# First half's final rows between products, row factors in two steps, and the second half's output projection in one piece

## The chip, the cores and the metric

The kernel runs on one core of a Trainium2 chip. The metric is the device time of one execution in microseconds (us). In the texts PE is the matrix engine (TensorE), PEld its loading of stationary operands, DVE the vector engine, ACT the scalar engine, POOL GpSimd, and SP the engine whose queue issues nearly all DMAs. A name such as L1216 is a line of the kernel before.

## What is computed

One step of a decoder layer on 1024 prompt tokens and 64 sample tokens (8 sequences of 8), 1088 tokens in all, with 1024 features, in float32:

```
xn   = rmsnorm(x, g_mix);  proj = xn @ w_in
S, o_g = gla_chunked(...)              # 4 heads of gated linear attention, 512 columns
o_g  = rmsnorm(o_g, g_gla) * silu(r)
o_s  = dilated_prompt(...) / dilated_sample(...)   # 8 softmax heads, 512 columns
h    = x + concat([o_g, o_s]) @ w_out              # w_out is 1024 x 1024
hn   = rmsnorm(h, g_ffn)
y    = h + (silu(hn @ w_fg) * (hn @ w_fu)) @ w_fd  # hidden width 2816
out  = rmsnorm(y, g_final)
```

States and caches are returned too; the change doesn't touch them.

## The kernel before

Every float32 product is made of three products of operands that are split into a high part (ACT copies with rounding, L172) and a low part (DVE subtracts, L173): hi by hi, lo by hi and hi by lo. So each weight that arrives by DMA takes an ACT and a DVE instruction before PE can use it. Tokens lie in the columns of products. They are cut into halves of 544 and pieces of `NH` = 272.

The order of instructions on each engine is not the order in which they are written. A scheduler places them by its own estimate of when operands are there and by priorities: `tc.high_priority()` pulls work forward, `fill_now` and `fill_behind` push work back by `LOW`. Buffers belong to rings: `pool.tile(..., tag=..., bufs=n)` hands out n buffers in turn, and the next user of a buffer waits until the last reader of the one before is done. Within an engine, instructions run in order, so that one that waits holds all that stands behind it. The names at each stage:

- **The filler.** `stream()` is a generator that yields after every group of products. First come 264 steps of six products of the input projection; then the GLA half of the output projection (rows 0 to 511 of w_out, L477 loads two column blocks of 128 at a time), in 48 steps of six products: 8 feature blocks, three token pieces of 384, 384 and 320 (`CHUNKS`), two steps each. Their sum with x goes back to `x_dram` in DRAM (L518, L519), through a ring `xa` of four. `FILL_AT` says how many steps are to be done at the end of each of the four attention pairs, and `FILL_ALL` how many there are.
- **The attention pairs** (`attn_pair`, four of them, the last from about 595 us). PE's own work for a pair is a chain through ACT and DVE; the steps of the filler stand between. The filler's 48 output steps all run from 600 to 705 us.
- **`out_half(hf)`** adds rows 512 to 1023 of w_out for one half of the tokens. It reads the attention output from `o_dram` (`load_rows`, L1027), splits it, takes four loads of w_out, and for 8 feature blocks by two token pieces makes 12 products into a bank of PSUM, which DVE adds to `xa`, read back from `x_dram` (L1041, L1046). For half 0 the sum stays in SBUF as `h[0]`, for half 1 it goes back to `x_dram`.
- **`factors(hf, ...)`** makes the row factors of the RMS norm: five products with one column (L1065), a chain of small DVE operations (`rms`, `rsqrt`), a broadcast into `rows`, five transposes on PE (L1073) and two copies into `rstd_bc`. `norm_half(hf)` multiplies h by them and builds the sums and splits `xhi`, `xlo` (tiles `B` and `T`) that the gate products read.
- **The 22 rounds** (`calls`, 11 of each half): `gate_up` makes seven blocks M1 to M7 of 24 products each (L1216, into banks `ps_a`, `ps_b`, `ps_c`), for which `gate_up_weights` loads four raw weight tiles A11, A21, A22, A12 and has POOL make the sums S1 to S4 (L1104), all out of the ring `raw` of seven buffers of 4 KB for each partition; `down` makes 96 products (L201 to L203, `ps_d`) and DVE adds them to `h`. The weights of `down` (`wd_raw`) use the single buffer `wraw`.
- **`final_rows(hf, t0, m)`** writes the final norm of 128 tokens: eight transposes of h into `ps_y` (a bank of the two of `ps_b`, L1294), a copy to `y` by ACT (L1295), the sum of squares by ACT (L1297), twelve small DVE operations on `st`, a product by DVE (L1299) and the DMA (L1300). `y` is the single buffer `wraw`. The first half's five calls stand behind the whole twelfth round, as does the load of `h[1]` (L1344).

Of the kernel before, what the change touches and what calls it, by code (L numbers as in the profile page):

```python
# [11 lines left out]
F32 = mybir.dt.float32  # L12
F32R = mybir.dt.float32r
# [6 lines left out]
P = 128  # L20
D = 1024
KT = D // P
# [16 lines left out]
FILL_AT = (156, 199, 242, 273, 306)  # L39
# [4 lines left out]
FILL_ALL = 312  # L44
# [59 lines left out]
def hymba_layer(  # L104
# [32 lines left out]
    def bank(tag):  # L137
        return psum.tile([P, 512], F32, tag=tag, name=f"ps_{tag}", bufs=1 if tag in "AX" else 2)
# [319 lines left out]
    def load_o(pl, c, half):  # L458
        c0, n = CHUNKS[c]
        hi = pl.tile([P, 4, 384], F32R, tag="ohi", name="ohi", bufs=3)  # L460
        lo = pl.tile([P, 4, 384], F32R, tag="olo", name="olo", bufs=3)
        oraw = pl.tile([P, 4, 384], F32, tag="oraw", name="oraw", bufs=2)
        dma(out=oraw[:, :, :n], in_=o_dram[512 * half : 512 * half + 512, c0 : c0 + n].rearrange("(k p) t -> p k t", p=P))
        for k in range(4):
            split(hi[:, k, :n], lo[:, k, :n], oraw[:, k, :n])
        return [hi[:, k, :n] for k in range(4)], [lo[:, k, :n] for k in range(4)]
# [17 lines left out]
    def stream():  # L484
# [21 lines left out]
        os = [load_o(outg, c, 0) for c in range(3)]  # L506
        for f in range(KT):
            if f % 2 == 0:
                ws, after = after, load_w_out(f + 2, 0) if f + 2 < KT else None
            for c, (c0, n) in enumerate(CHUNKS):  # L510
                cs = slice(c0, c0 + n)
                xa = outg.tile([P, 384], F32, tag="xa", name="xa", bufs=4)[:, :n]
                dma(out=xa, in_=x_dram[:, f, cs])
                ps = bank("mm")[:, :n]
                for k in (0, 2):
                    mm3(ps, [part[k : k + 2] for part in ws[f % 2]], [o[k : k + 2] for o in os[c]], first=k == 0, last=k == 2)
# [505 lines left out]
    def load_rows(c0):  # L1022
        hi = outp.tile([P, 4, NH], F32R, tag="ohi", name="ohi", bufs=4)
        lo = outp.tile([P, 4, NH], F32R, tag="olo", name="olo", bufs=4)
        for k in range(0, 4, 2):
            oraw = outp.tile([P, 2, NH], F32, tag="oraw", name="oraw", bufs=3)
            dma(out=oraw, in_=o_dram[512 + k * P : 512 + (k + 2) * P, c0 : c0 + NH].rearrange("(k p) t -> p k t", p=P))  # L1027
            split(hi[:, k : k + 2], lo[:, k : k + 2], oraw)
        return [hi[:, k] for k in range(4)], [lo[:, k] for k in range(4)]

    def out_half(hf):
        os = [load_rows(2 * NH * hf + NH * n) for n in range(2)]
        sq_acc = outp.tile([P, 2 * NH], F32, name="acc") if hf == 0 else None
        for f in range(KT):
            if f % 2 == 0:
                ws = load_w_out(f, 1)
            for n in range(2):
                cs = slice(NH * n, NH * n + NH)
                xs = x_dram[:, f, 2 * NH * hf + NH * n : 2 * NH * hf + NH * n + NH]
                xa = outp.tile([P, NH], F32, tag="xa", name="xa", bufs=3)  # L1040
                dma(out=xa, in_=xs)  # L1041
                ps = bank(("mm", "S", "T")[(2 * f + n) % 3])[:, :NH]
                mm3(ps, ws[f % 2], os[n])
# [5 lines left out]
                if hf:  # L1049
                    pass  # L1050
                elif f == 0:
                    act(out=sq_acc[:, cs], in_=row, func=AF.Square)
                else:
                    sq = outp.tile([P, NH], F32, tag="sq", name="sq", bufs=2)
                    act(out=sq, in_=row, func=AF.Square)
                    pool.tensor_tensor(out=sq_acc[:, cs], in0=sq_acc[:, cs], in1=sq, op=ALU.add)
        return sq_acc

    def factors(hf, sq_acc, ps, rb):
# [11 lines left out]
        vec.tensor_copy(out=rows, in_=st[:, 1, :].unsqueeze(2).broadcast_to([P, len(tiles), P]))  # L1071
        for j, m in tiles:
            nc.tensor.transpose(out=rb[j // 4][:, j % 4 * P : j % 4 * P + m], in_=rows[:m, j, :], identity=ident[:m, :m])  # L1073
# [100 lines left out]
    def gate_up(xs, own, following, wd):  # L1174
# [33 lines left out]
        for j, (name, _, slot, bk, first) in enumerate(ORDER):  # L1208
# [63 lines left out]
    factors(0, sums, bank("A"), [bank("X"), bank("A")])  # L1272
# [11 lines left out]
    def final_rows(hf, t0, m):  # L1284
# [3 lines left out]
        y = wpool.tile([P, KT, P], F32, tag="wraw", name="y", bufs=1).rearrange("p (f k) c -> p f (k c)", f=2)  # L1288
# [12 lines left out]

    calls = [(hf, i) for hf in range(2) for i in range(NF // 2)]
# [8 lines left out]
    for call, (hf, i) in enumerate(calls):  # L1311
        following = gate_up_weights(calls[call + 1][1]) if call + 1 < len(calls) else None
        B = gate_up(xs, own, following, load)
# [26 lines left out]
        if (hf, i) == (1, 0):  # L1340
            for t0 in range(0, 2 * NH, P):
                final_rows(0, t0, min(P, 2 * NH - t0))
            h[1] = residual()
            dma(out=h[1], in_=x_dram[:, :, 2 * NH :])  # L1344
# [96 lines left out]
```

## Time and profile before

| | us |
|---|---|
| median of 3 runs (lowest, highest) | 1628.04 (1627.64, 1631.65) |
| the profiled execution | 1630.76 |
| its span | 1629.0 |
| PE busy in the span | 1490.5 |
| DVE, ACT, POOL busy | 987.9, 590.3, 584.1 |
| mean granted clock of PE | 0.958 |

A busy time of PE counts matmuls that overlap, and a matmul at the lower clock counts for longer, so that 92% of the span is not 92% of what PE can do. More is learned from stretches of the span: which engine is busy in each, what the granted clock was, and for what PE waited there. The profile's rounds of the steady part are 33.2 us long and PE never stops in them; the rest of the text is about the stretches where it does.

### The profile page before, as it was taken

The numbers are of one execution on the slowest core, as the hardware profiler recorded it, in microseconds if no ns is written. First come the engines' busy times: TensorE is split into PE (matmuls) and PEld (weight loads), VectorE is DVE, ScalarE is ACT, GpSimd is POOL, SyncE is SP. The second block draws the span as 40 slices with busy tenths as digits, with TensorE's granted clock in tenths as the row PEclk, the third lists the DMA queues.
The fourth block names the chain that finished last, engine by engine and source line by source line (L and its number), as shares of the span: only waits on it lengthen the run. The fifth ranks groups of instructions, "written<-read, shape, count | busy, mean of one in ns | idle before, by whom it ended". The sixth has DMA issues, their size and how long they took to land.

```text
span 1629.0 us, 32149 instructions
## 1 busy us (share of the span) xinstructions
PE 1490.5 (92%) x13363; PEld 1338.2 (82%) x13363; DVE 987.9 (61%) x1673; ACT 590.3 (36%) x1002; POOL 584.1 (36%) x413
## 2 busy tenths in 40 slices
PE   7979999999999998978699999999884799999995
PEld 6867877887676766778589999999884799999995
DVE  5495675633323243246586787776975577767755
ACT  3243332243433444223443433333343243333432
POOL 1493332131121000033684453544642155544521
PEclk9988999999999999989799999999997899999997
DMA  4320021263534466575342322332413323323301
GB/s 151 102 71 27 25 67 43 56 197 105 141 103 123 123 182 197 163 239 175 110 144 78 102 81 87 108 92 78 133 53 119 107 91 106 102 79 104 91 27 55
DMA packets 237746, 172.58 MB, mean 106 GB/s; under 512 B 17792, under 2 KB 224032, under 8 KB 237600
## 3 DMA queue, kind: packets, MB, share of 16 engines
q1 hardware_dynamic: 233392, 170.31, 34.9%
q8 instruction: 105, 1.72, 0.4%
q10 hardware_dynamic: 4208, 0.21, 0.2%
q14 instruction: 41, 0.34, 0.1%
HBM read 144.79 MB, written 25.69 MB: 105 GB/s over the span
## 4 chain that ended last, share of the span: by engine, by line
PE 71%; DVE 12%; DMA 9%; ACT 2%; POOL 2%; issue 2%; SPq 1%; ACTq 0%; DVEq 0%; POOLq 0%
PE ps_b L1216 11%; PE ps_a L1216 6%; PE ps_c L1216 6%; PE ps_mm L201 6%; PE ps_mm L203 6%; PE ps_mm L202 6%; PE ps_d L201 5%; PE ps_d L203 5%; PE ps_d L202 5%; PE ps_S L840 2%; DMA x_dram<-xa 2%; DVE wlo L173 2%; PE ps_X L982 1%; PE ps_T L938 1%; DMA out_dram<-y 1%
## 5 line engine op out<-in xcount | busy, mean ns | idle before, releaser
L1104 POOL TENSOR_TENSOR raw<-raw 128x1024 f32<-128x1024 f32 x88 | 260.1, 2964 | 433.7 <-DVE wlo L173 280.1
L172 ACT ACTIVATE whi<-raw 128x1024 fp32r<-128x1024 f32 x154 | 162.9, 1058 | 240.3 <-PE ps_a L1216 87.0
L173 DVE TENSOR_TENSOR wlo<-raw,whi 128x1024 fp32r<-128x1024 f32 x154 | 242.2, 1575 | 0.0
L201 PE MATMUL ps_d<-ghi,wdhi 128*128 128x272 f32 (+2 forms) x704 | 205.5, 294 | 16.3 <-ACT wdhi L172 9.4
L202 PE MATMUL ps_d<-glo,wdhi 128*128 128x272 f32 (+2 forms) x704 | 205.6, 293 | 1.1 <-DVE glo L173 1.1
L201 PE MATMUL ps_mm<-xhi,whi 128*128 128x384 f32 (+1 forms) x576 | 199.4, 347 | 2.0 <-ACT whi L172 1.6
L203 PE MATMUL ps_d<-ghi,wdlo 128*128 128x272 f32 (+2 forms) x704 | 201.2, 292 | 0.0
L203 PE MATMUL ps_mm<-xhi,wlo 128*128 128x384 f32 (+1 forms) x576 | 195.1, 340 | 1.0 <-DVE wlo L173 1.0
L202 PE MATMUL ps_mm<-xlo,whi 128*128 128x384 f32 (+1 forms) x576 | 195.1, 339 | 0.2 <-DVE xlo L278 0.2
L1216 PE MATMUL ps_b<-xhi,whi 128*128 128x272 f32 x528 | 156.7, 297 | 18.5 <-ACT y L1295 11.3
L1216 PE MATMUL ps_b<-xhi,wlo 128*128 128x272 f32 x528 | 158.1, 299 | 5.6 <-DVE wlo L173 5.6
L1216 PE MATMUL ps_b<-xlo,whi 128*128 128x272 f32 x528 | 156.2, 296 | 2.4 <-DVE xlo L173 2.4
L201 PEld LDWEIGHTS ps_d<-ghi,wdhi 128*128 128x128 f32 x704 | 135.1, 192 | 18.2 <-ACT wdhi L172 11.6
L202 PEld LDWEIGHTS ps_d<-glo,wdhi 128*128 128x128 f32 x704 | 135.8, 193 | 1.5 <-DVE glo L173 1.5
L203 PEld LDWEIGHTS ps_d<-ghi,wdlo 128*128 128x128 f32 x704 | 133.4, 192 | 0.0
L201 PEld LDWEIGHTS ps_mm<-xhi,whi 128*128 128x128 f32 x576 | 110.7, 192 | 12.2 <-issue 7.3
L1216 PEld LDWEIGHTS ps_b<-xhi,whi 128*128 128x128 f32 x528 | 103.4, 196 | 20.2 <-ACT y L1295 11.8
L1266 DVE TENSOR_TENSOR h<-h,ps_d 128x544 f32<-128x544 f32 x168 | 113.7, 711 | 9.8 <-PE ps_d L203 9.8
L1216 PE MATMUL ps_a<-xhi,whi 128*128 128x272 f32 x352 | 102.7, 292 | 16.2 <-DVE xa L1046 10.1
L203 PEld LDWEIGHTS ps_mm<-xhi,wlo 128*128 128x128 f32 x576 | 110.4, 192 | 7.3 <-issue 5.3
L202 PEld LDWEIGHTS ps_mm<-xlo,whi 128*128 128x128 f32 x576 | 110.9, 193 | 6.3 <-issue 5.3
L1216 PEld LDWEIGHTS ps_b<-xhi,wlo 128*128 128x128 f32 x528 | 103.3, 196 | 7.9 <-DVE wlo L173 6.9
(363 smaller groups left out, 3453.2 us busy)
## 6 DMA issues: line engine op xcount, KB each, us to landing
raw<-in_w_ffn_gate_dram SPq DMA_DIRECT2D x88, 256.0 KB, 3.1
raw<-in_w_ffn_up_dram SPq DMA_DIRECT2D x88, 256.0 KB, 3.4
wd_raw<-in_w_ffn_down_dram SPq DMA_DIRECT2D x44, 512.0 KB, 3.8
wraw<-in_w_in_dram SPq DMA_DIRECT2D x22, 512.0 KB, 3.8
raw<-in_cache_swa_k_dram SPq DMA_DIRECT2D x32, 256.0 KB, 4.8
raw<-in_cache_swa_v_dram SPq DMA_DIRECT2D x32, 256.0 KB, 3.6
wraw<-in_w_out_dram SPq DMA_DIRECT2D x12, 512.0 KB, 4.0
xa<-x_dram SPq DMA_DIRECT2D x32, 136.0 KB, 2.7
```

The source lines that it names most:

```text
L172: a = by.tensor_copy(out=hi, in_=raw) if by else act(out=hi, in_=raw, func=AF.Copy)
L173: return a, vec.tensor_tensor(out=lo, in0=raw, in1=hi.bitcast(F32), op=ALU.subtract)
L201: mm(out=ps, lhsT=whi[k], rhs=xhi[k], start=first and k == 0, stop=False)
L202: mm(out=ps, lhsT=whi[k], rhs=xlo[k], start=False, stop=False)
L203: mm(out=ps, lhsT=wlo[k], rhs=xhi[k], start=False, stop=last and k == n - 1)
L840: ins = mm(out=out, lhsT=qres[own, qi * P + 32 * r : qi * P + 32 * r + 32], rhs=rhs, start=True, stop=True)
L938: nc.tensor.transpose(out=ps[:, r * P : (r + 1) * P], in_=raw[:, r, :], identity=ident)
L982: mm(out=av[rs, b2 * P : (b2 + 1) * P], lhsT=pT[:, t, rs], rhs=vts[b2][:, r, :], start=False, stop=t == 5 and b2 == 1)
L1104: add = lambda out, a, b, op: pool.tensor_tensor(out=out, in0=raw[a], in1=raw[b], op=op)
L1216: mm(out=banks[bk][:, s], lhsT=l[:, k, s], rhs=r, start=first and k == 0 and a == 0, stop=k == n - 1 and a == 2, skip_group_check=not first)
L1266: ins = vec.tensor_tensor(out=hk, in0=hk, in1=ps, op=ALU.add)
```

## The change

1. The filler's output steps cover only the first half of the tokens: two pieces of 272 instead of three, so 32 steps instead of 48 (`FILL_ALL` 312 to 296, `FILL_AT` with it). Its ring `xa` grows from four to six.
2. `out_half(1)` contracts all 1024 rows of w_out in one go: 24 products into a bank instead of 12, w_out by eight loads of 128 columns (`load_w`) instead of four of half the rows and 256 columns. `out_half`'s `xa` ring grows from three to six, and the tiles of `load_rows` are pairs in rings of nine.
3. `factors` ends with the broadcast `rows`; the transposes and copies are a new function `spread`. For the second half `factors` is called behind round 5 (counted from 0) and `spread` behind round 6.
4. `y` of `final_rows` comes from the ring `raw` of seven. The first half's final rows are called between the blocks of the second half's first two rounds: behind blocks 1, 3 and 5 of round 11, and behind blocks 0 and 2 of round 12; `h[1]` is loaded behind block 3 of it.

The diff, cut to its core:

```diff
-FILL_AT = (156, 199, 242, 273, 306)
+FILL_AT = (156, 194, 230, 264, 288)
-FILL_ALL = 312
+FILL_ALL = 296
...
-        os = [load_o(outg, c, 0) for c in range(3)]
+        os = [load_o(outg, n, 0) for n in range(2)]
...
-            for c, (c0, n) in enumerate(CHUNKS):
-                cs = slice(c0, c0 + n)
-                xa = outg.tile([P, 384], F32, tag="xa", name="xa", bufs=4)[:, :n]
+            for n in range(2):
+                cs = slice(NH * n, NH * n + NH)
+                xa = outg.tile([P, NH], F32, tag="xa", name="xa", bufs=6)
...
+    def load_rows(c0, ks):
+        pairs = []
+        for k in ks:
+            hi = outp.tile([P, 2, NH], F32R, tag="ohi", name="ohi", bufs=9)
+            lo = outp.tile([P, 2, NH], F32R, tag="olo", name="olo", bufs=9)
+            oraw = outp.tile([P, 2, NH], F32, tag="oraw", name="oraw", bufs=2)
...
+        os = [load_rows(2 * NH * hf + NH * n, range(0 if hf else 4, KT, 2)) for n in range(2)]
...
-            if f % 2 == 0:
-                ws = load_w_out(f, 1)
+            if hf:
+                parts = load_w(w_out[:, f * P : (f + 1) * P])
+                w = [[part[:, k] for k in range(KT)] for part in parts]
+            else:
+                if f % 2 == 0:
+                    ws = load_w_out(f, 1)
+                w = ws[f % 2]
...
-                xa = outp.tile([P, NH], F32, tag="xa", name="xa", bufs=3)
+                xa = outp.tile([P, NH], F32, tag="xa", name="xa", bufs=6)
...
-    def factors(hf, sq_acc, ps, rb):
+    def factors(hf, sq_acc, ps):
...
+        return rows
+
+    def spread(hf, rows, rb):
...
+            if j in between:
+                between[j]()
...
-        y = wpool.tile([P, KT, P], F32, tag="wraw", name="y", bufs=1).rearrange("p (f k) c -> p f (k c)", f=2)
+        y = ffp.tile([P, KT * P], F32, tag="raw", name="y", bufs=7).rearrange("p (f c) -> p f c", f=2)
...
-        B = gate_up(xs, own, following, load)
+        B = gate_up(xs, own, following, load, {
+            NF // 2: {j: lambda t=t: final_rows(0, P * t, P) for t, j in enumerate((1, 3, 5))},
+            NF // 2 + 1: {0: lambda: final_rows(0, 3 * P, P), 2: lambda: final_rows(0, 4 * P, 2 * NH - 4 * P), 3: next_rows},
+        }.get(call, {}))
...
         if call == 5:
+            factor_rows = factors(1, sums, psum2.tile([P, 2, 512], F32, tag="b", name="ps_f", bufs=2)[:, 0])
+        if call == 6:
             ps = psum2.tile([P, 2, 512], F32, tag="b", name="ps_f", bufs=2)
-            factors(1, sums, psum2.tile([P, 2, 512], F32, tag="b", name="ps_f", bufs=2)[:, 0], [ps[:, 0], ps[:, 1]])
+            spread(1, factor_rows, [ps[:, 0], ps[:, 1]])
```

How the change moves instructions is seen at three places. The first is DVE at the end of `out_half(1)`, where `xa<-ps` are the additions of the output projection (L1046, now L1053), `xlo` the low parts of the operands of the gate products, and `wlo` those of weights (from `raw`, for the gate; from `wraw`, for the output projection). Before:

```order
L1046 TENSOR_TENSOR xa<-ps_T,xa 128x272
L1168 SCALAR_TENSOR_TENSOR B<-h,gf,rstd_bc 128x2x272
L1168 SCALAR_TENSOR_TENSOR B<-h,gf,rstd_bc 128x544
L1046 TENSOR_TENSOR xa<-ps_mm,xa 128x272
L173 TENSOR_TENSOR xlo<-T,xhi 128x1088
L173 TENSOR_TENSOR xlo<-B,xhi 128x816
L1287 MEMSET st 128x4 x2
L1354 MEMSET one 128x1
L1389 MEMSET st_last 128x12
L173 TENSOR_TENSOR wlo<-raw,whi 128x1024
L173 TENSOR_TENSOR wdlo<-wd_raw,wdhi 128x1024
L173 TENSOR_TENSOR xlo<-T,xhi 128x1088 x2
```

After:

```order
L173 TENSOR_TENSOR xlo<-T,xhi 128x1088
L1053 TENSOR_TENSOR xa<-ps_S,xa 128x272
L173 TENSOR_TENSOR wlo<-wraw,whi 128x1024
L1053 TENSOR_TENSOR xa<-ps_T,xa 128x272
L173 TENSOR_TENSOR xlo<-T,xhi 128x1088
L1053 TENSOR_TENSOR xa<-ps_mm,xa 128x272
L173 TENSOR_TENSOR wlo<-wraw,whi 128x1024
L1053 TENSOR_TENSOR xa<-ps_S,xa 128x272
L173 TENSOR_TENSOR wlo<-raw,whi 128x1024
L1053 TENSOR_TENSOR xa<-ps_T,xa 128x272
L1053 TENSOR_TENSOR xa<-ps_mm,xa 128x272
L173 TENSOR_TENSOR wlo<-raw,whi 128x1024
```

Before, four low parts `xlo` stand behind the last addition of the output projection; after, four additions stand behind the last `xlo`.

The second is ACT in the second half's first rounds, where `y<-ps_y` and `T,st<-y` are the copy and the squares of final rows, `s<-ps_a` belongs to block M1, `B<-` to the blocks behind it, and `whi` to weights. Before:

```order
L1186 ACTIVATE s_13414<-ps_a 128x544
L172 ACTIVATE ghi<-B 128x544
L172 ACTIVATE whi<-raw 128x1024
L1295 ACTIVATE y<-ps_y 128x1024
L1297 ACTIVATE T,st<-y 128x1024
L1295 ACTIVATE y<-ps_y 128x1024
L1297 ACTIVATE T,st<-y 128x1024
L172 ACTIVATE whi<-raw 128x1024
L1295 ACTIVATE y<-ps_y 32x1024
L1297 ACTIVATE T,st<-y 32x1024
```

After:

```order
L1306 ACTIVATE y<-ps_y 128x1024
L1189 ACTIVATE B<-u_13127 128x272
L1308 ACTIVATE T,st<-y 128x1024
L172 ACTIVATE whi<-raw 128x1024 x2
L1189 ACTIVATE B<-s_13126 128x272
L1306 ACTIVATE y<-ps_y 128x1024
L172 ACTIVATE ghi<-B 128x544 x2
L1308 ACTIVATE T,st<-y 128x1024
L1306 ACTIVATE y<-ps_y 128x1024
L172 ACTIVATE whi<-raw 128x1024
L1195 ACTIVATE s_13454<-ps_a 128x544
L1308 ACTIVATE T,st<-y 128x1024
```

Before, three of the final rows' copies come in one run, with their squares and a single weight split between them; after, splits and blocks' copies stand between one copy and the next, and squares no longer follow their copy at once.

The third is the DMA queue (SP) at the same place: `out_dram<-y` are the final rows, `h<-x_dram` the load of the second half, `raw` and `wd_raw` weights. Before:

```order
L1102 DMA raw<-in_w_ffn_gate_dram 128x4x128
L1102 DMA raw<-in_w_ffn_up_dram 128x4x128
L1300 DMA out_dram<-y 128x1024
L1344 DMA h<-x_dram 128x8x544
L1300 DMA out_dram<-y 128x1024 x2
L1102 DMA raw<-in_w_ffn_gate_dram 128x4x128
L1102 DMA raw<-in_w_ffn_up_dram 128x4x128
L1102 DMA raw<-in_w_ffn_gate_dram 128x4x128
L1102 DMA raw<-in_w_ffn_up_dram 128x4x128
L1102 DMA raw<-in_w_ffn_gate_dram 128x4x128
L1102 DMA raw<-in_w_ffn_up_dram 128x4x128
L1300 DMA out_dram<-y 32x1024
```

After:

```order
L1111 DMA raw<-in_w_ffn_gate_dram 128x4x128
L1111 DMA raw<-in_w_ffn_up_dram 128x4x128
L1311 DMA out_dram<-y 128x1024 x2
L1315 DMA h<-x_dram 128x8x544
L1111 DMA raw<-in_w_ffn_gate_dram 128x4x128
L1111 DMA raw<-in_w_ffn_up_dram 128x4x128
L1111 DMA raw<-in_w_ffn_gate_dram 128x4x128
L1111 DMA raw<-in_w_ffn_up_dram 128x4x128
L1253 DMA wd_raw<-in_w_ffn_down_dram 128x1024
L1111 DMA raw<-in_w_ffn_gate_dram 128x4x128
L1111 DMA raw<-in_w_ffn_up_dram 128x4x128
L1311 DMA out_dram<-y 128x1024
```

Before, the loads of `wd_raw` come only behind the last of these rows; after, they lie among the final rows' DMAs. The load of h now has four weight loads and a load of `wd_raw` directly behind it, where two DMAs of final rows stood.

## Rows read from the trace of the kernel before

**Rows 1.** The page, 40 slices of the span: busy tenths of PE in each slice.

```profile
PE   7979999999999998978699999999884799999995
```

**Rows 2.** Stretches: length; busy us (count) of PE, PEld, DVE, ACT, POOL; clock; DMA; GB/s.

```profile
514.40:595.10 80.70, 80.07 (x832) 58.04 (x832) 24.85 (x77) 33.73 (x70) 7.07 (x9) 1.00 0.47 133
595.10:705.30 110.20, 102.08 (x929) 77.64 (x929) 38.54 (x116) 41.45 (x93) 0.00 (x0) 0.97 0.67 199
...
769.10:802.50 33.40, 15.56 (x65) 13.86 (x65) 21.66 (x26) 12.39 (x13) 14.57 (x13) 0.64 0.43 124
...
1184.70:1292.00 107.30, 70.56 (x475) 66.56 (x474) 69.14 (x116) 35.84 (x48) 31.43 (x18) 0.84 0.31 101
1292.00:1325.20 33.20, 33.19 (x265) 32.97 (x264) 23.61 (x25) 12.39 (x17) 15.56 (x7) 1.00 0.33 96
```

**Rows 3.** Timeline of PE: start, length, line, operation; six products of the filler.

```profile
701.86 0.34 PE L201 MATMUL ps_mm<-ohi,whi 128*128 128x384 f32 x1
...
702.90 0.34 PE L201 MATMUL ps_mm<-ohi,whi 128*128 128x384 f32 x1
```

**Rows 4.** Waits of PE after attention: total, times, longest.

```profile
PE ps_mm L201 <- ACT ohi L172: 7.4, 1, 7.4
```

**Rows 5.** Timeline of PE from the factors of the first half to its gate products.

```profile
756.95 0.66 PE L1073 MATMUL ps_X<-ident,T 128*128 128x128 f32 x4 [0.82 <-DVE T L1071]
...
779.21 0.56 PE L1216 MATMUL ps_a<-xhi,whi 128*128 128x272 f32 x1 [10.09 <-DVE xa L1046]
...
797.90 0.59 PE L1216 MATMUL ps_b<-xlo,whi 128*128 128x272 f32 x1 [0.51 <-DVE xlo L173]
```

**Rows 6.** Timeline of the DMA queue (w_out loads), and the page's part 6.

```profile
729.24 0.38 SPq L477 DMA_DIRECT2D wraw<-in_w_out_dram  x1
...
754.83 0.38 SPq L477 DMA_DIRECT2D wraw<-in_w_out_dram  x1
...
wraw<-in_w_in_dram SPq DMA_DIRECT2D x22, 512.0 KB, 3.8
wraw<-in_w_out_dram SPq DMA_DIRECT2D x12, 512.0 KB, 4.0
```

**Rows 7.** Waits of PE and of ACT from 1184 to 1292 us.

```profile
PE ps_b L1216 <- ACT y L1295: 11.3, 1, 11.3
PE ps_d L201 <- ACT wdhi L172: 9.4, 2, 6.7
...
ACT y L1295 <- DMA out_dram<-y: 23.3, 4, 11.0
```

**Rows 8.** Timeline of DVE in final rows; the page's row of POOL.

```profile
1204.84 2.31 DVE L158 SCALAR_TENSOR_TENSOR st<-st 128x1 f32<-128x1 f32 x1
1207.18 3.33 DVE L1299 SCALAR_TENSOR_TENSOR y<-y,st,gfin 128x1024 f32<-128x1024 f32 x1
...
1224.63 0.16 DVE L158 SCALAR_TENSOR_TENSOR st<-st 128x1 f32<-128x1 f32 x1
1224.82 1.28 DVE L1299 SCALAR_TENSOR_TENSOR y<-y,st,gfin 128x1024 f32<-128x1024 f32 x1
...
L1104 POOL TENSOR_TENSOR raw<-raw 128x1024 f32<-128x1024 f32 x88 | 260.1, 2964 | 433.7 <-DVE wlo L173 280.1
```

**Rows 9.** Timelines of ACT, DVE and the DMA queue at the end.

```profile
1607.48 0.19 ACT L1297 ACTIVATION_READ_ACCUMULATOR T<-y 128x1 f32 x1
1614.80 1.02 ACT L1295 ACTIVATE y<-ps_y 96x1024 f32<-96x1024 f32 x1 [0.46 <-DMA out_dram<-y]
...
1623.75 0.69 ACT L1404 ACTIVATE y<-ps_y,st_last 128x512 f32<-128x512 f32 x1 [6.75 <-DMA out_dram<-y]
...
1613.81 1.40 DVE L1405 TENSOR_SCALAR y<-ps_y,st_last 128x512 f32<-128x512 f32 x2 [0.81 <-ACT y L1404]
...
1625.25 0.34 SPq L1407 DMA_DIRECT2D out_dram<-y  x1
```

**Rows 10.** Waits of PE round the factors of the second half.

```profile
PE ps_d L201 <- DVE B L1181: 2.1, 1, 2.1
```

More of the change, by code (lines that the diff above doesn't have):

```diff
@@ L456, in hymba_layer, with load_o @@
     jobs += values_of(1) + gates_of(0) + raws_of(0) + gates_of(1) + raws_of(1) + raws_of(2) + raws_of(3)
[L458 to L463, printed above, removed]
+    def load_o(pl, n, half):
+        hi = pl.tile([P, 4, NH], F32R, tag="ohi", name="ohi", bufs=2)
+        lo = pl.tile([P, 4, NH], F32R, tag="olo", name="olo", bufs=2)
+        oraw = pl.tile([P, 4, NH], F32, tag="oraw", name="oraw", bufs=2)
+        dma(out=oraw, in_=o_dram[512 * half : 512 * half + 512, n * NH : n * NH + NH].rearrange("(k p) t -> p k t", p=P))
         for k in range(4):
-            split(hi[:, k, :n], lo[:, k, :n], oraw[:, k, :n])
-        return [hi[:, k, :n] for k in range(4)], [lo[:, k, :n] for k in range(4)]
+            split(hi[:, k], lo[:, k], oraw[:, k])
+        return [hi[:, k] for k in range(4)], [lo[:, k] for k in range(4)]
     def load_w_out(f, half):
@@ L509, in stream @@
                 ws, after = after, load_w_out(f + 2, 0) if f + 2 < KT else None
[L510 to L512 removed]
+            for n in range(2):
+                cs = slice(NH * n, NH * n + NH)
+                xa = outg.tile([P, NH], F32, tag="xa", name="xa", bufs=6)
                 dma(out=xa, in_=x_dram[:, f, cs])
[L514 removed]
+                ps = bank("mm")[:, :NH]
                 for k in (0, 2):
[L516 removed]
+                    mm3(ps, [part[k : k + 2] for part in ws[f % 2]], [o[k : k + 2] for o in os[n]], first=k == 0, last=k == 2)
                     if k == 2:
@@ L1020, in hymba_layer @@
     vec.memset(ones, 1.0)
[L1022 to L1029, printed above, removed]
+    def load_rows(c0, ks):
[4 more added lines that the diff above has]
+            oraw = outp.tile([P, 2, NH], F32, tag="oraw", name="oraw", bufs=2)
+            dma(out=oraw, in_=o_dram[k * P : (k + 2) * P, c0 : c0 + NH].rearrange("(k p) t -> p k t", p=P))
+            split(hi, lo, oraw)
+            pairs.append((hi, lo))
+        return [[pair[part][:, k] for pair in pairs for k in range(2)] for part in range(2)]
     def out_half(hf):
-        os = [load_rows(2 * NH * hf + NH * n) for n in range(2)]
-        sq_acc = outp.tile([P, 2 * NH], F32, name="acc") if hf == 0 else None
+        os = [load_rows(2 * NH * hf + NH * n, range(0 if hf else 4, KT, 2)) for n in range(2)]
+        sq_acc = None if hf else outp.tile([P, 2 * NH], F32, name="acc")
         for f in range(KT):
-            if f % 2 == 0:
-                ws = load_w_out(f, 1)
+            if hf:
[5 more added lines that the diff above has]
+                w = ws[f % 2]
             for n in range(2):
@@ L1071, in factors @@
         vec.tensor_copy(out=rows, in_=st[:, 1, :].unsqueeze(2).broadcast_to([P, len(tiles), P]))
+        return rows
+    def spread(hf, rows, rb):
+        tiles = [(j, min(P, 2 * NH - j * P)) for j in range(-(-2 * NH // P))]
         for j, m in tiles:
@@ L1172, in norm_half, with gate_up @@
         return xs
-    def gate_up(xs, own, following, wd):
+    def gate_up(xs, own, following, wd, between={}):
         s1, u2, v5 = temps()
@@ L1271, in hymba_layer @@
     sums = out_half(0)
-    factors(0, sums, bank("A"), [bank("X"), bank("A")])
+    spread(0, factors(0, sums, bank("A")), [bank("X"), bank("A")])
     xs = norm_half(0)
@@ L1300, in final_rows, with next_rows @@
         dma(out=out_rows(t0, m), in_=y[:m])
+    def next_rows():
+        h[1] = residual()
+        dma(out=h[1], in_=x_dram[:, :, 2 * NH :])
     calls = [(hf, i) for hf in range(2) for i in range(NF // 2)]
@@ L1339, in hymba_layer @@
             load = None
[L1340 to L1344, printed above, removed]
     for j in range(2):
```

4 lines of the change are left out of this document (1 added, 3 removed).

## The prediction

> **What bounds the kernel now.** I read the page's slices first [rows 1]: PE is at nines nearly everywhere, so PE sets the time, except in a few slices that show where it stands idle. Then the table of stretches [rows 2], which gives the price of each. In a steady round PE is busy for 33.19 of 33.20 us, and 264 products make it, so a product of 272 columns costs 33.2 / 264 = 0.1257 us. Against that price three stretches lose time. From 769.1 to 802.5 us only 65 products run, worth 8.2 us: 25.2 us are lost between the output projection and the gate products. From 1184.7 to 1292.0 us two rounds' gate blocks and one down block run, 336 + 96 = 432 products worth 54.3 us, with 40 transposes (four took 0.66 us [rows 5], so 6.6 us): 61 us of work in 107.3 us, 46 us lost. The rest is the end of the program [rows 9]. The clock was 0.64 and 0.84 of full in the two holes: PE falls to its lower level, 1.2 GHz, when it has been idle, and pays for that as well.
>
> The waits say what ends last in each hole. In the first PE waits 10.09 us, then in small pieces for `xlo`, the last at 797.90 us [rows 5]: the norm's operands are late while there is no other product to make. In the second PE waits 11.3 us for the copy of `y`, and ACT itself waits 23.3 us in four waits for the DMA that empties `y`'s one buffer; the down weights, which share it, cost 9.4 us more [rows 7].
>
> **A. The output projection is moved.** The filler's 48 steps run in the last pair's stretch, where PE is busy for 102.08 of 110.20 us [rows 2]. Six products of 384 columns take 702.90 - 701.86 = 1.04 us [rows 3]; by columns six of 320 take 0.87. So 32 x 1.04 + 16 x 0.87 = 47.2 us leave, and 32 x 6 x 0.1257 = 24.1 us come: -23.1. Behind the attention `out_half(1)` gets 16 x 12 products more, 24.1 us. PE's work is therefore the same; what is gained is that the 24.1 us now lie where PE had nothing to do. By the order some 295 of its products, 37.1 us, stand behind the transposes of the first half's factors, and the last `xlo` comes ahead of the last four additions, where before four `xlo` came behind the last one. In the trace the operands were complete 797.90 - 756.95 = 41.0 us behind those transposes [rows 5]. So PE is covered but for some 4 us, and the first gate blocks need only the first operands: I leave 2 of the 25.2 us standing (at worst 9, if ACT and DVE are later and the clock drops).
>
> What can eat this: the last pair loses 23 us of cover for its own chain. Pair 2 ran in 80.70 us with 80.07 busy, so a chain fits in that time; the last pair would have 102.1 - 23.1 = 79 us of work. I add 4 us of idle (0 to 8). The 7.4 us for the last attention rows [rows 4] stay: the change leaves that path as it is. Sum: -23.1 + 24.1 + 4 - 25.2 + 2 = **-18**, from -24 (no idle, nothing left) to -7 (8 and 9).
>
> The added instructions: four more loads of w_out, each with a split by ACT and DVE; pairs of attention rows, 8 to 12 (half 1 reads all 1024 rows); of the filler's 24 additions into `xa` 16 smaller ones remain. All that lies beside PE. The loads set a pace: five issues from 729.24 to 754.83 us, 6.40 us each, against 48 x 0.1257 = 6.03 of products for one load, the same 48 after as before. Eight loads fall 3 us behind at most, which is in the 9. The new loads have rows of 512 B in place of 1 KB; loads of w_in of that shape took 3.8 us where w_out's took 4.0 [rows 6], so I add nothing. The Trainium skill (DMA: Bandwidth & Descriptors, Why small descriptors are slow) gives each packet a fixed overhead of three cycles; by its figures 512 B would cost about 9% more for the same bytes, an estimate of 0.3 us a load and some 3 us over eight. The trace doesn't show that, and the measurement decides.
>
> **B. Factors in two steps.** Round 5's down products wait 2.1 us for `B` behind the small DVE operations [rows 10]. These operations stay in the same place; only five transposes and two copies move a round later. **0**, from -3 (the wait and the dip go) to +2 (another one comes).
>
> **C. Final rows between products.** Each of five takes with it eight transposes, a copy and a square on ACT, twelve small DVE operations of 0.16 us at about 0.2 apart, a product of 1.28 us when undisturbed [rows 8], and a DMA; then comes h's load. Nothing is added in sum; what goes is the single buffer: the 11.3 and 9.4 us of PE and the clock that they cost. New is that `y` takes a slot of the ring of seven, and holds it until its DMA has landed. Who waits for that: POOL's sum S2 of round 12 goes into the first row's slot, and POOL, in order, holds everything behind it; ACT's split of S2 waits for POOL, with a copy of `y` behind; the load of h waits for the last transposes, and weight loads for round 13 are queued behind it on SP. The floor is PE's 61 us. DVE was busy 69.1 us in this stretch [rows 2], and that holds some stretched operations: a small one took 2.31 us and one product 3.33 us. With DVE that close I take 67 us: **-40**, from -46 (61 us) to -25 (82 us, next paragraph but one).
>
> **D. The end.** The second final row's copy by ACT waits until 1614.80 us although ACT's last square was done at 1607.67; the third row's waits 6.75 us until 1623.75, all for `y`'s buffer [rows 9]. Without that the third piece follows the second half of DVE's work at 1613.81 + 1.40 = 1615.2, plus its own 0.75 and an issue: about 1617 in place of 1625.25. **-8.3**, from -10 to -6.
>
> Everything else: 0, from -4 to +4. **Sum**: -18 + 0 - 40 - 8.3 = -66. The profiled execution took 1630.76 us (1.76 beyond its span), so it becomes 1564.5; the median of the runs is 2.7 lower, 1628.04, and gives **1562 us**.
>
> **Rivals.** *DVE becomes the bound in the two rounds.* POOL's weight sums take 2.96 us each, and DVE's two-operand instructions beside them were the stretched ones [rows 8]. If every row's product waits out one POOL sum, 5 x 2.96 = 14.8 us come on top of 67: 82 us, and the sum is -51: 1577. For: DVE's 69 us exceed PE's 61. Against: POOL was busy for 31 of 107 us, so not every product meets a sum. The Trainium skill (SBUF — State Buffer, Who interferes with whom) states a lock: a DVE instruction with two SBUF inputs and a GpSimd instruction that reads SBUF exclude each other for the whole instruction. The trace agrees: 1.28 us free, 3.33 us beside a sum.
>
> *The attention doesn't shrink.* If the last pairs' chains need the time whatever fills it, all 23.1 us come back as idle in place of 4: A is +1, the sum -47: 1581. For: the 8.1 us of idle that the last pair already has. Against: pair 2's 80.7 us.
>
> *The change doesn't close the first hole.* Four more splits of weights stand between the norm's operations on ACT and DVE; if `xlo` comes 14 us later, the hole remains by as much: 1576.
>
> *Slower: the ring starves.* If each `y` is next in line for a load or a sum that PE needs, PE waits for the whole way of a slot: the `y` DMA (up to 11.0 us of ACT's wait [rows 7]), a load (3.8), a POOL sum (2.96), some 18 us. Five times 18 on 61 us is 151 us, +44 instead of -40: sum +18, 1646. It makes the kernel slower by over 0.3% (5 us) only if more than some 16 us per row stay uncovered. Against: seven slots, of which `y` takes one at a time, and loads a round ahead.
>
> **How the numbers follow.** Forecast 0.55; DVE as the bound 0.20; attention 0.11; first hole 0.08; starving ring 0.03; two of them together 0.03. Range: down to 1544 (A -24, C -46, D -10, the rest -4) and up to 1584, which holds each of the first three rivals alone. What a measurement of this kernel can tell from no change is about 0.3%, 5 us. Faster 0.95: all but the starving ring and a mix of small shares; same 0.02; slower 0.03.
>
> **What would show it.** Right: the last pair's stretch some 19 us shorter at near full busy share; gate products starting within 3 us of the output projection's last; the two rounds in 62 to 72 us with no wait of ACT for `y`'s DMA; the last DMA 8 us earlier behind PE's end. Wrong: waits in the last pair above 10 us; a stretch from the second half's first block to steady rounds of over 80 us with DVE at nines, or with POOL waiting for `out_dram<-y`; a new wait in pairs 0 to 2, which get five and seven steps less and three more.

## The result, and the profile after

The changed kernel takes 1571.15 us in the median of four runs (1566.48 to 1576.16), the kernel before 1629.52 beside it: a ratio of 0.9642, with an interval from 0.9608 to 0.9676, or 58 us less (53 to 64). The prediction was 1562 us with a range from 1544 to 1584. The profiled execution took 1570.21 us, its span 1568.4, which is 60.6 less than before. This text's accounts are of the two spans.

The page's slices of the changed kernel, to be held against [rows 1]:

```profile
PE   6979999999999999969889999999988999999996
```

Of the second hole's slices 8, 8, 4 and 7 two slices of 8 are left. Where the first hole had 7, 8 and 6, two slices of 8 are left and, ahead of them, one of 6 (667 to 706 us), which holds the wait behind the last attention pair.

To divide the gain I use one instruction that every round has once, ACT's copy `s<-ps_a` behind block M1 (start, length, line, operation). Rounds 2, 10 and 14 of the 22, counted from 0, in the kernel before:

```profile
862.82 0.60 ACT L1186 ACTIVATE s<-ps_a 128x544 f32<-128x544 f32 x1
...
1137.22 0.61 ACT L1186 ACTIVATE s<-ps_a 128x544 f32<-128x544 f32 x1
...
1332.03 0.61 ACT L1186 ACTIVATE s<-ps_a 128x544 f32<-128x544 f32 x1
```

and in the changed one:

```profile
845.78 0.61 ACT L1195 ACTIVATE s<-ps_a 128x544 f32<-128x544 f32 x1
...
1117.60 0.61 ACT L1195 ACTIVATE s<-ps_a 128x544 f32<-128x544 f32 x1
...
1278.01 0.61 ACT L1195 ACTIVATE s<-ps_a 128x544 f32<-128x544 f32 x1
```

Round 2 starts 17.04 us earlier, round 10 19.62, round 14 54.02, the end of the span 60.6. So the first 17.0 us are gained ahead of round 2 (term A), 2.6 round the factors (B), 34.4 from round 10 to round 14, which holds the final rows (C), and 6.6 at the end (D). The prediction had 18, 0, 40 and 8.3. These are differences of one pair of traces; the experiments show how far each can be trusted.

Three stretches of the changed kernel, with the columns of [rows 2]: the last attention pair, from the end of the pair before; the time in which PE waits for the last attention rows; and the two rounds with the final rows, cut as the 107.3 us of [rows 2] were:

```profile
590.40:670.00 79.60, 74.88 (x808) 50.91 (x802) 29.28 (x100) 40.49 (x91) 2.79 (x5) 0.96 0.64 188
...
675.00:685.30 10.30, 0.37 (x3) 0.15 (x2) 1.67 (x2) 1.71 (x2) 3.80 (x2) 0.67 1.00 308
1165.60:1240.00 74.40, 65.31 (x488) 63.12 (x488) 63.08 (x113) 34.94 (x47) 27.66 (x17) 0.95 0.39 126
```

The two rounds take 74.4 us in place of 107.3. This cut holds 13 matmuls more than that of the kernel before (488 against 475), some 1.6 us, so that 107.3 less the 34.4 of the marks, 72.9 us, is the figure to compare. PE's waits in them (total, times, longest) are no longer those of [rows 7]:

```profile
PE ps_a L1225 <- DVE h L1277: 3.8, 2, 3.3
PE ps_a L1225 <- DVE B L1190: 3.5, 1, 3.5
PE ps_b L1225 <- DVE xlo L173: 0.8, 1, 0.8
```

No wait for `y` is among them. PE's two longest waits are for DVE, some 3.4 us each. The one for `B` isn't new; PE had it in the same stretch of the kernel before (1184 to 1292 us), beside the waits of [rows 7]:

```profile
PE ps_a L1216 <- DVE B L1181: 3.8, 1, 3.8
```

It ended when DVE came through the stretched operations of [rows 8].

### The profile page after: what moved, and what is told of

Same layout as the page of the kernel before. It is cut to its first block, busy times and chain, and to the rows that moved or that the text cites. A ratio compares the mean times of both kernels' runs of the same rounds, so it can differ in the third digit from the quotient of the medians.

```text
span 1568.4 us, 32306 instructions
## 1 busy us (share of the span) xinstructions
PE 1476.7 (94%) x13459; PEld 1328.9 (85%) x13459; DVE 989.7 (63%) x1669; ACT 593.1 (38%) x1006; POOL 587.3 (37%) x413
```

## The experiments

The place of each gain is read by the same marks: the start of round 2, the time from round 10's mark to round 14's (194.8 us before, 160.4 after), and what is left to the end. Ahead of round 2 the profiles of kernels with the same edits there differ by up to 6 us (its mark stands at 842.0 to 848.4), while steady rounds repeat to some 0.05 us; so differences of a few us there are given as a spread over several profiles. The stretch from round 10 to round 14 varies too: six profiles with the changed kernel's final rows took 159.5 to 162.3 us there, so that less than 3 us between two profiles of it says little.

### Each part by itself

```diff
 e1_a_alone: edits 1 and 2 of the change, on the kernel before
-FILL_AT = (156, 199, 242, 273, 306)
+FILL_AT = (156, 194, 230, 264, 288)
...
+                parts = load_w(w_out[:, f * P : (f + 1) * P])
```

> The kernel before with the first two edits alone (the filler's output steps for the first half only, out_half(1) over all rows of w_out); row factors, final rows and the tail as before. Theory (PE's work is the same, 24 us of it moves into the hole ahead of the gate products): 17 us less than before, all of it gained before round 2, and nothing changes behind it. Rival (the last attention pairs need their time whatever fills it): 0 to 3 us less. Rival (the places depend on each other and the four gains don't add up): something else than 14 to 20 us less.

Measured: 1612.47 us, ratio 0.9898 (0.9868 to 0.9928), 17 us less (12 to 22). Round 2's mark stands at 845.6 us, 17.2 earlier than before, and from round 10 to round 14 it takes 195.0 us, as before. The moved products are worth this by themselves, and behind them nothing changes but 1.5 us in the rounds from 5 to 8, which vary by as much (below). Edits 1 and 2 also bring larger rings and other tiles of attention rows; these were not tried apart from the moved products.

```diff
 e2_c_alone: the final rows' edits, on the kernel before
-        y = wpool.tile([P, KT, P], F32, tag="wraw", name="y", bufs=1)...
+        y = ffp.tile([P, KT * P], F32, tag="raw", name="y", bufs=7)...
...
+            if j in between:
+                between[j]()
```

> The kernel before with the final rows' edits alone (y from the ring of seven, the first half's final rows between the products of rounds 11 and 12, h's load there too). Theory: 34 us less in rounds 11 to 13 and 6.6 less at the end, 41 in all. If the gains don't add up: outside 37 to 45 us.

Measured: 1588.5 us, ratio 0.9755 (0.9736 to 0.9774), 40 us less (37 to 43). From round 10 to 14 it takes 158.9 us, 35.9 less, and 6.9 are gained behind the last rounds. The parts add up: 17 and 40 against 58.

### The ring or the place

```diff
 e3_ring_only: on the kernel before
-        y = wpool.tile([P, KT, P], F32, tag="wraw", name="y", bufs=1)...
+        y = ffp.tile([P, KT * P], F32, tag="raw", name="y", bufs=7)...
```

> The kernel before with y taken from the ring of seven, the final rows still called in one run behind round 11. Theory (the single buffer was the cause of most of the hole; where the rows are called matters less): 6.6 us less at the end and 20 to 30 less in rounds 11 to 13, so 27 to 37 in all. Rival (it takes the place between the products): 6.6 less at the end, at most 8 less in the rounds, 7 to 15 in all.

```diff
 e5_no_ring: the changed kernel, but
+        y = wpool.tile([P, KT, P], F32, tag="wraw", name="y", bufs=1)...
-        y = ffp.tile([P, KT * P], F32, tag="raw", name="y", bufs=7)...
```

> The changed kernel with y in the single buffer as before: the final rows of the first half stand between products, but share one buffer with each other and with the down weights. Theory (the buffer is what costs): PE again waits for the DMA of y, 20 to 32 us more than the changed kernel in rounds 11 to 13 and 6.6 more at the end. Rival (rows some 12 us apart find the buffer free): 6.6 at the end and at most 8 in the rounds.

Measured: the ring alone gives 1591.15 us, ratio 0.9771 (0.9751 to 0.9792), 37 less than before. The place without the ring, with edits 1 to 3, gives 1601.91, ratio 0.9824 (0.9804 to 0.9844). From round 10 to round 14:

| | rows in one run | rows between products |
|---|---|---|
| single buffer | 194.8 | 185.1 |
| ring of seven | 163.8 | 160.4 (158.9 without edits 1 to 3) |

The ring is worth 31.0 us where the rows stand in one run, and 24.7 where they stand between products; the place is worth 9.7 without the ring; with it the first traces give 3.4 to 4.9, and the spread of 158.9 to 162.3 over all profiles 1.5 to 4.9. The single buffer was the cause of most of the hole. Waits of PE (total, times, longest) from 1130 us with the ring alone show what it took away: of the 11.3 us for `y` in [rows 7] 1.3 are left, and a DVE operation is now the longest:

```profile
PE ps_d L201 <- DVE s L1184: 4.9, 1, 4.9
...
PE ps_b L1216 <- ACT y L1295: 1.3, 1, 1.3
```

Waits of PE, and then of ACT, from 1110 us with the place alone: the down weights, which share the buffer, wait again, and PE for them:

```profile
PE ps_d L201 <- ACT wdhi L172: 8.0, 2, 4.5
PE ps_b L1225 <- DVE st L1298: 4.8, 2, 4.6
```

```profile
ACT wdhi L172 <- DMA wd_raw<-in_w_ffn_down_dram: 24.4, 6, 12.9
...
ACT y L1306 <- DMA out_dram<-y: 11.8, 3, 8.5
```

Behind round 21's mark the ring alone gave 6.9 us, and without it 6.5 of the changed kernel's gain were lost.

### The factors in two steps

```diff
 e4_no_b: the changed kernel, but
-            factor_rows = factors(1, sums, ...)
-        if call == 6:
-            spread(1, factor_rows, [ps[:, 0], ps[:, 1]])
+            factors(1, sums, ..., [ps[:, 0], ps[:, 1]])
```

> The changed kernel with the row factors of the second half in one step as before. Theory (the step in two took away 2.6 us round the factors): 2 to 4 us more than the changed kernel. Rival (that difference of the two traces is a chance of how the rounds fall): no more than 1 us either way. A few us are near what runs of the changed kernel differ by (1566 to 1576), so the place in the trace decides: rounds 5 to 7 take 72.5 us there before, 69.5 after.

Measured: 1569.84 us, ratio 0.9638 (0.9621 to 0.9656), the same as the changed kernel. From round 5's mark to round 8's it took 108.0 us here. But these rounds are not the same in every profile of one program: five profiles with factors in one step took 106.4 to 108.0, nine with two steps 105.4 to 106.9, the changed kernel itself once 105.4 and once 106.9. The 2.6 us that the first pair of traces showed are mostly chance; about 1 us may be real, and the times don't show it.

### What the moved products cost where they now stand

```diff
 e8_leave_out: the changed kernel, but
-                mm3(ps, w, os[n])
+                mm3(ps, [p[4:] for p in w] if hf else w, [o[4:] for o in os[n]] if hf else os[n])
```

> The changed kernel with the 192 products of the first 512 rows of w_out left out of out_half(1) (their loads and splits stay): 24.1 us less work for PE ahead of the gate products. Theory (those products lie where PE has to wait for the norm's operands anyhow): the gate products start hardly earlier, 0 to 5 us less than the changed kernel. Rival (they lie on the path as they did in the attention stretch): 18 to 24 us less.

Measured: 1565.62 us, ratio 0.9604 (0.9583 to 0.9625), 5.5 us less than the changed kernel's median for 24.1 us less of products. Round 2's mark:

```profile
839.22 0.61 ACT L1195 ACTIVATE s<-ps_a 128x544 f32<-128x544 f32 x1
```

That is 6.6 us earlier than in the changed kernel's first profile. From the transposes of the first half's factors to this mark it took 108.4 us, against 111.7 to 117.1 in the profiles with the products (and 105.9 to 106.4 in those of the kernel before's order, where these 24.1 us stood in the attention). So most of the 24.1 us lie beside other work, as the theory said, but not as nearly all as the prediction had it. The 108.4 us are still 2 us above the order of before, with the products gone and only their loads and splits left: the products cost 3 to 9 us here, the weights for them some 2 (one profile).

### The last attention pair and the wait behind it

```diff
 e7_fill280: the changed kernel, but
-FILL_AT = (156, 194, 230, 264, 288)
+FILL_AT = (156, 194, 230, 264, 280)
```

> The changed kernel with eight more of the filler's steps (6.0 us of products) left for behind the last attention pair, where PE waits 10 us for the last attention rows. Theory (the last pair's own chain takes less than its time with 24 steps): the pair gets 5 to 6 us shorter, its idle time stays near 5 us, and the wait of 10 us falls to some 4: 4 to 6 us less. Rival (the last pair's chain sets its time): the pair's idle grows by as much and nothing is gained, 0 to 1 us.

Measured: 1575.86 us, ratio 0.9664 (0.9637 to 0.9690), no gain. The last pair's stretch (columns of [rows 2]), and PE's wait for the attention rows behind it:

```profile
594.50:673.20 78.70, 73.14 (x794) 49.17 (x791) 28.84 (x100) 39.60 (x90) 2.78 (x5) 0.96 0.63 181
```

```profile
PE ps_mm L201 <- ACT ohi L172: 7.0, 1, 7.0
```

The pair got no more than 0.9 us shorter than the changed kernel's 79.60. The wait fell from 10.0 to 7.0 us, but the time from the pair's end to PE's start on the new rows stayed at 15.6 (15.3). The gain is nothing, as the rival had it. Its cause, that this pair's chain sets its time, is not shown: of the 48 products that the edit allows behind the pair only some 14 left its stretch (808 matmuls before, 794 here), 1.7 us of work, of which 0.9 came off.

```diff
 e10_later_loads: the changed kernel, but
+    with after_all([marks[3]]):
         own[0]()
 (marks are the loads of attention rows in load_rows)
```

> The changed kernel with the first round's eight gate and up loads (256 KB each) issued behind out_half(0)'s four loads of attention rows, instead of some 10 us ahead of them. Theory (the 10 us wait of PE behind the last attention pair is the time of the DMA engines, which are busy for 1.00 of it with gate weights that are needed 90 us later): the wait falls to 3 to 6 us, 4 to 8 us less in all. Rival (it is the path of the last pair: write of osT, read back, split): the wait stays at 9 to 10 us, within 1 us of the changed kernel.

Measured: 1570.06 us, ratio 0.9616 (0.9591 to 0.9641), the same. PE's waits from 660 to 830 us:

```profile
PE ps_mm L203 <- DVE wlo L173: 5.7, 4, 2.4
PE ps_mm L201 <- ACT ohi L172: 4.5, 1, 4.5
```

The wait for attention rows did fall to 4.5 us, but PE now waits 5.7 us for low parts of weights, and from the pair's end to the factors' transposes it takes 57.7 us, against 56.0 to 59.0 in the profiles with the changed kernel's order of loads. My reading, which no further run tests: the transfers, which keep the DMA engines busy for all of the wait in the changed kernel (share 1.00 in its table of stretches), all have to go through before PE can go on; in another order another one is last. Neither theory had that.

### DVE's small operations

```diff
 e6_no_newton: the changed kernel, but, for the first half's final rows
-        for _ in range(3):
+        for _ in range(steps):        # 0 there
```

> The changed kernel without the nine small DVE operations (three steps of the inverse root) of each of the first half's five final rows: 45 operations less, so that those rows come out with a rough factor. Theory (the two waits of 3.45 and 3.31 us in rounds 11 and 12 are DVE's, which in order gets through small operations that are stretched beside POOL's sums): 5 to 9 us less than the changed kernel, both waits gone. Rival (PE waits there for something else that DVE's rows only happen to stand beside): 0 to 2 us less.

Measured: 1565.84 us, ratio 0.9602 (0.9586 to 0.9619). From round 10 to round 14 it took 156.6 us, 3.8 less than the changed kernel (5 to 9 were expected) and 2.9 less than the lowest of the six profiles; the wait for `B` is gone, and the longest for `h` fell from 3.3 to 1.0 us. So the small operations cause these waits. The timeline of the changed kernel shows how; DVE (start, length, line, operation) ahead of the addition into `B`, for which PE waits 3.45 us:

```profile
1183.90 0.15 DVE L154 TENSOR_SCALAR st<-st 128x1 int32<-128x1 int32 x1
1184.09 1.77 DVE L156 TENSOR_TENSOR st<-st 128x1 f32<-128x1 f32 x1
1185.89 0.70 DVE L157 SCALAR_TENSOR_TENSOR st<-st 128x1 f32<-128x1 f32 x1
1186.62 2.29 DVE L158 SCALAR_TENSOR_TENSOR st<-st 128x1 f32<-128x1 f32 x1
1188.95 0.16 DVE L156 TENSOR_TENSOR st<-st 128x1 f32<-128x1 f32 x1
...
1190.11 1.28 DVE L1310 SCALAR_TENSOR_TENSOR y<-y,st,gfin 128x1024 f32<-128x1024 f32 x1
1191.31 0.43 DVE L1190 TENSOR_TENSOR B<-B,ps_a 128x272 f32<-128x272 f32 x1
```

and POOL at that time:

```profile
1183.45 2.39 POOL L1113 TENSOR_TENSOR raw<-raw 128x1024 f32<-128x1024 f32 x1 [11.59 <-DVE wlo L173]
1185.79 0.78 POOL L1190 TENSOR_TENSOR B<-B,v 128x272 f32<-128x272 f32 x1
1186.52 2.37 POOL L1113 TENSOR_TENSOR raw<-raw 128x1024 f32<-128x1024 f32 x1
```

DVE's operation from 1184.09 ends at 1185.86, POOL's product from 1183.45 at 1185.84; the next of DVE at 1186.59, POOL's second at 1186.57; the third at 1188.91, POOL's third at 1188.89. Each small operation with two operands ends with the POOL instruction beside which it began, and takes 0.70 to 2.29 us in place of 0.16. The operation with one operand at 1183.90, beside the same POOL product, took 0.15. The addition stands behind all of it on DVE. The Trainium skill (SBUF — State Buffer, Who interferes with whom) states that a DVE instruction with two SBUF inputs contends with a GpSimd instruction that reads SBUF, and has the contention as an exclusive lock on a shared pair of ports; the rows agree, to 0.02 us. The wait for `h` comes about in the same way: a small operation from 1232.13 us takes 2.28, until POOL's second of two sums is done at 1234.40, and the additions into `h` stand behind it.

```diff
 e9_poolchain: the changed kernel, but, for the first half's final rows
-            vec.tensor_tensor(out=t, in0=y, in1=y, op=ALU.mult)
+            pool.tensor_tensor(out=t, in0=y, in1=y, op=ALU.mult)
 (and the rest of a step with it, in four operations)
```

> The changed kernel with the three steps of the inverse root of the first half's final rows on POOL (twelve small operations a row) instead of DVE (nine). Theory (DVE, in order, holds the adds that PE waits for while its small operations are stretched beside POOL's sums): on POOL they can't stand beside a sum, so both waits of 3.4 us go, 3 to 5 us less than the changed kernel in rounds 11 to 13. Rival (it is the length of a row's chain, not the engine): POOL takes as long or longer with it and holds its own sums, 0 to 6 us more.

Measured: 1574.94 us, ratio 0.9649 (0.9628 to 0.9669). Both waits for DVE are gone, and two others came (PE, from 1165 us):

```profile
PE ps_b L1230 <- ACT whi L177: 7.5, 1, 7.5
PE ps_b L1230 <- DVE wlo L178: 1.9, 2, 1.6
```

From round 10 to 14 it took 163.3 us, 2.9 more than the changed kernel's first profile and 1.0 more than the highest of the six. ACT's split for the 7.5 us stands behind copies of `y` (DVE, then ACT):

```profile
1202.48 1.28 DVE L1315 SCALAR_TENSOR_TENSOR y<-y,st,gfin 128x1024 f32<-128x1024 f32 x1 [1.72 <-POOL st L159]
...
1207.51 1.94 ACT L1311 ACTIVATE y<-ps_y 128x1024 f32<-128x1024 f32 x2 [6.95 <-DMA out_dram<-y]
1209.33 2.00 ACT L177 ACTIVATE whi<-raw 128x1024 fp32r<-128x1024 f32 x2
```

A row's product on DVE now waits for POOL. That of the first row comes 16.0 us behind the first copy of `y`, where it was 9.9 in the changed kernel, and its DMA later with it. The third copy then waits 6.95 us for the second row's DMA, and ACT, in order, holds the weight's split behind it. So the wait moved to the slots of the ring: the prediction's starving ring, which the changed kernel itself escapes. The rival had the size (0 to 6 us more) and a longer chain, but not this way.

```diff
 e11_eight_ops: the changed kernel, but, for the first half's final rows
-        rms(st[:, 1:2], st[:, 0:1], D, st[:, 2:3])
...
+            for _ in range(2):
+                vec.scalar_tensor_tensor(out=t, in0=y1, scalar=half, in1=y1, op0=ALU.mult, op1=ALU.mult)
+                vec.scalar_tensor_tensor(out=y1, in0=t, scalar=1.5, in1=y1, op0=ALU.add, op1=ALU.mult)
```

> The changed kernel with the factor of each of the first half's final rows in eight small DVE operations instead of twelve (two steps of the inverse root instead of three, with two operations a step). Theory (DVE's small operations, stretched beside POOL's sums, hold the adds behind them; without nine of them the rounds were 3.8 us shorter): about four ninths of that, 1 to 3 us less than the changed kernel measured beside it, in rounds 11 to 13. Rival (only the row as a whole matters): within 0.5 us in those rounds.

> The changed kernel as it is, beside the one with eight operations on the same chip. Both theories: 1566 to 1576 us, and in the trace waits of 3.3 to 3.5 us in rounds 11 and 12 in the same places as before; the time of a run differs by what happens ahead of the rounds, up to 4 us.

Measured, side by side: eight operations 1571.57 us (1569.26 to 1578.57, ratio 0.9631, 0.9613 to 0.9649), the changed kernel 1568.69 (1568.04 to 1571.79, ratio 0.9622, 0.9603 to 0.9641). Fewer operations brought nothing. Waits of PE in the two rounds with eight operations, and then in the changed kernel's second profile:

```profile
PE ps_d L201 <- DVE h L1277: 4.5, 1, 4.5
PE ps_a L1225 <- DVE B L1190: 2.5, 1, 2.5
```

```profile
PE ps_a L1225 <- DVE B L1190: 3.5, 1, 3.5
PE ps_a L1225 <- DVE h L1277: 3.0, 1, 3.0
```

The changed kernel's waits came back in the same places with 3.5 and 3.0 us. With eight operations they are 2.5 and 4.5, and the four rounds took 165.1 us (161.4 in the changed kernel beside it; the profiled execution with eight was the longest of its six, by 5 us). Neither theory came true. In this trace a row's operations fell beside three of POOL's sums in one run,

```profile
1230.75 7.59 POOL L1113 TENSOR_TENSOR raw<-raw 128x1024 f32<-128x1024 f32 x3 [1.46 <-DMA raw<-in_w_ffn_gate_dram]
```

and all four with two operands took longer: 1.37, 1.93, 2.30 and 0.68 us, with the additions into `h` behind them. My theory that the loss goes with the number of operations falls; what these traces point to instead, and no run tests, is which of them meet a POOL sum with an addition for PE behind them. No version tried is faster than the changed kernel, but for the two that leave work out.

## Why the prediction was right, and where not

**What bounds the kernel** was read rightly: two holes and the end, 25 and 46 us and the waits for `y`. The parts tried alone add up to the whole, and the gains of C and D lie where the prediction put them; A's came by other terms than it named.

**A, -18 forecast, -17.0 measured: the sum was right, but by luck; its terms were not.** Over the profiles, from the end of one pair to the next mark:

| us | order of before (3 profiles) | edits 1 and 2 | forecast |
|---|---|---|---|
| end of pair 2 | 595.2 to 597.7 | 589.6 to 595.4 | no change |
| last pair | 105.0 to 107.3 | 78.5 to 80.6 | 19 less |
| to PE's start on the new rows | 11.0 to 11.5 | 13.6 to 15.5 | no change |
| to the transposes of the factors | 43.8 to 44.2 | 42.4 to 44.0 | no change |
| to round 2 | 105.9 to 106.4 | 111.7 to 117.1 | 1 more |

(The second column leaves out e7 and e10, which change this stretch, and in its last row e8.) I had added 4 us of idle to the last pair; it has 4.7 in all, 79.60 less 74.88, where it had 8.1. So it lost some 26 us, not 19; why it has less idle time with less cover is not shown. Against this, the wait behind it grew by some 3 us; the loads of gate weights have a share in that wait, since it is 4.5 us with them issued later (e10). And the hole ahead of the gate products closed by less than forecast. I left 2 us standing of 25.2. But 24.1 us of products made that stretch 5 to 11 us longer, where the forecast had 1. The step that failed is "PE is covered but for some 4 us": products and weights for them wait in this stretch, as in PE's waits of the changed kernel from 728 to 846 us,

```profile
PE ps_b L1225 <- DVE wlo L173: 3.5, 3, 2.7
PE ps_mm L201 <- ACT whi L172: 1.5, 2, 1.3
```

Some 6 to 12 of the 25.2 us were left, round the 9 that I had as the worst case, and the last pair paid it back. Which of the splits and loads is late there was not separated further.

Two more things make -17.0 less firm than it looks. The first line of the table is not the work of the edits alone: attention's first product stands at 335.2 us in the changed kernel's first profile and at 339.3 in that of before, but at 334.6 to 340.3 in others with the same edits, so that 4 us of the 17.0 arose there, within that spread. By the means of the profiles (three and eight) round 2 comes 19 us earlier. And nothing was added for the new loads, but the time from issue to landing rose (median; before, 3.8 for w_in and 4.0 for w_out [rows 6]):

```profile
wraw<-in_w_in_dram SPq DMA_DIRECT2D x22, 512.0 KB, 4.2
wraw<-in_w_out_dram SPq DMA_DIRECT2D x16, 512.0 KB, 4.7
```

The loads of w_in, which are as before, take longer as well, so whether the shorter rows have a part in it is not shown.

**B, 0 forecast, 2.6 in the first traces**, and by e4 and the repeats about 1: the forecast stands.

**C, -40 forecast, -34.4 measured.** The cause was right (the single buffer, 31 of it by e3). What was mis-sized is the 67 us for the two rounds: 72.9, cut alike. I took them between PE's 61 us and DVE's 69. DVE ended with 63.1 of 74.4 us busy, so it isn't full, and yet PE waits for it: not for its sum of work, but for additions that stand behind a row's small operations, stretched by POOL. The 3.8 us of e6 are the larger part of the 5.6 that are missing; the rest was not separated. The rows of before could have told: PE's wait of 3.8 us for `B` was there, and the prediction counted only the waits for `y` and the down weights. The rival of DVE as the bound named the right two engines, and had 82 us; what happened lies between it and the forecast, with the small operations in the place of the large product, which took 1.28 us undisturbed. The ring did not starve: PE's list has no wait for a weight of the ring above 0.2 us there, though POOL's sums waited for a `y`'s DMA (1165 to 1245 us), and e9 shows how near it was:

```profile
POOL raw L1113 <- DMA out_dram<-y: 6.0, 2, 5.4
```

**D, -8.3 forecast, -6.6 measured.** `y`'s buffer is no longer waited for: the last row's pieces follow one another (ACT), and the last DMA is issued at 1563.14 us.

```profile
1559.14 1.83 ACT L1419 ACTIVATE y<-ps_y,st_last 128x512 f32<-128x512 f32 x3 [3.40 <-DVE st L158]
```

```profile
1563.14 0.53 SPq L1422 DMA_DIRECT2D out_dram<-y  x1
```

From round 21's mark (1564.96 us before, 1510.93 after) that is 52.2 us against 60.3 with the 1625.25 of [rows 9], 8.1 less: the step "about 1617" was right. What the sum left out lies behind the issue. From there to the end of the span it takes 5.3 us in place of 3.7. Three DMAs of 256 to 512 KB are now issued within 1.3 us, where before the last stood alone, which may be why; the last one's time to landing (DMA issues from 1555 us: KB, us) is

```profile
out_dram<-y SPq DMA_DIRECT2D x1, 256.0 KB, 4.3
```

**The range** held, and no rival came true as a whole. That the sum came within 9 us is in part luck, by A's terms above. The miss of 9 us against the point is C's 5.6, D's 1.7 and A's 1.0, less B's 2.6, and 3.7 because the profiled execution stood 2.7 us above the median before and 0.9 below it after.

## What to carry to other kernels

Ask first what buffer a slow stretch shares, and only then where its work stands: a ring of seven in place of one buffer gave 31 us with nothing moved, and moving the rows as well added 1.5 to 5. Work that is taken out of a busy stretch into a hole is gained only as far as its own operands and weights arrive in the hole: 24 us of products cost 5 to 11 us there. And an engine that isn't full can still be the one that is waited for: look for what stands behind its longest instruction, not for its share of busy time. A chain that is moved to another engine to clear such a wait can end later there, and hold a buffer for longer.

## What the runs showed of the hardware

A DVE operation on 128 x 1 elements, 0.16 us by itself, took up to 2.29 us, and ended within 0.02 us of the POOL instruction beside it; I had expected this of the product of 1024 columns. With one operand it took 0.15 beside the same POOL instruction. Steady rounds of 33.2 to 33.3 us repeat from one profile to the next, while the changed kernel's two profiles differ by 5.1 us in when the last pair ends (670.0 and 675.1), so that a few us of one pair of traces ahead of the rounds mean nothing without repeats. And with the DMA engines at a share of 1.00, an order of loads that took 5.5 us from one wait gave as much to others.
